# A streaming encoder step on one core: the pair that is finished last stays on chip, three pairs are stored twice, and their splits move two products back

## The chip, the cores and the metric

The kernel runs on one core of one Trainium2 chip. The metric is the device time of one execution in microseconds (us). Five engines work side by side, each through its own queue in order: TensorE (PE) multiplies, VectorE (DVE) and ScalarE (ACT) do elementwise work, GpSimd (POOL) does elementwise work and issues transfers of its own, SyncE (SP) only issues transfers. An instruction that waits holds up everything behind it in its queue.

## The reference, cut to what matters

One layer over 640 tokens (512 of the prompt, 128 of the samples), model width 2048, all in float32. The change lies in the feed-forward part:

```
D_FF = -(-8 * D_MODEL // (3 * 256)) * 256        # 5632
h = rmsnorm(x, norm_ffn)
return x + (jax.nn.silu(h @ w_gate) * (h @ w_up)) @ w_down
```

The projection, the two kinds of attention and the output projection ahead of it are not touched.

## The kernel before

**Arithmetic.** Float32 values are multiplied as two rounded parts, hi and lo: ACT writes hi (a copy that rounds), DVE or POOL writes lo = value - hi (a *split*), and PE adds the three products hi·hi, lo·hi and hi·lo (`mm3`, lines 204 to 206). A weight block is split by line 195 (ACT) and 196 (DVE) into one of three pairs of buffers, so the split for a product can be made once PE is through the product three places ahead of it.

**A quartet.** A matrix product of 2 x 2 blocks is done in seven block products instead of eight (Strassen's scheme in Winograd's form). `quartet` loads four weight blocks on SP (line 933), forms their combinations (lines 946 and 948 on DVE, 951 and 960 on POOL) and yields the products in the order p1, p6, p7, p2, p5, p4, p3. They use the left-hand operand numbers ("which") 0, 1, 2, 4, 3, 5, 6. Line 970 adds the results up on DVE.

**FF1.** The 5632 columns are 22 *pairs* of 128-blocks. For each pair one quartet computes the gate and one the up projection. A product has 8 k-tiles, so 24 matmuls. Then lines 1057 to 1059 apply SiLU, 1063 multiplies gate and up, and 1067 to 1070 form the combinations, so that a pair has seven *parts*, one for each product of FF2. `store_part`, called after most products, takes one part: line 1011 writes hi into one of two scratch buffers `half`, 1013 makes lo in place, and 1014 and 1015 store both to `act_d` in DRAM. Pairs 1, 2 and 3 (`raw_pairs`) are not split here: line 1007 stores the part as it is to `first_d`.

**FF2.** There are 32 steps. Step t works on output blocks t % 8 and t % 8 + 8, and on the five or six pairs that are active: pair j is active for 8 steps from START[j] on (modulo 32). With five pairs a product has 15 matmuls and a step 105. The operands of a pair are loaded with line 977 (POOL) as soon as a buffer is free, from `act_d`. In the first eight steps lines 1100 and 1101 load the residual blocks (`x2_d`, shown as `x_d` in the profile). 62 buffers "S" of 640 columns hold all of that; in FF1 56 of them hold the operand h.

**Between FF1 and FF2.** Step 0 uses pairs 0 to 4. After each product of the last up quartet `free` gives back the eight buffers of h that it used, and starts loading that product's operands for step 0: pairs 1 to 3 from `first_d` (line 987, one transfer of 320 KB and one of 160 KB), which it splits at once (992 on ACT, 993 on DVE or POOL), and pairs 0 and 4 with line 977. Pair 21 is finished last and first used in step 23; its parts are split and stored by `store_part` after the products of step 0. Pairs 1 to 3 are needed again in the last steps: line 1093, emitted where they leave (steps 2, 3 and 5) but placed on SP as soon as an operand is split, stores their 21 operands to `act_d`.

**The order.** The program is emitted in this order, and a scheduler then sets the order within each engine. `keep_behind` adds order edges: instructions that were emitted inside a marked stretch (`behind`) stay after the last ACT instruction emitted ahead of it outside of such stretches.

Of the kernel before, what the change touches and what calls it, by code (L numbers as in the profile page):

```python
# [8 lines left out]
ALU = mybir.AluOpType  # L9
# [8 lines left out]
HT = 320  # L18
# [9 lines left out]
REL = 128  # L28
NPAIR = NFF // 2
STEPS = 32  # L30
START = [25, 27, 28, 30, 31, 1, 3, 4, 6, 7, 8, 9, 11, 12, 14, 15, 16, 17, 19, 20, 22, 23]


def active(step):

    return [j for j in range(NPAIR) if (step - START[j]) % STEPS < 8]
# [5 lines left out]
def f(ap):  # L42
    return ap.bitcast(F32)
# [6 lines left out]
class Net:  # L50


    def __init__(self, nc, tc, io, pools):
        self.nc, self.tc, self.io, self.pools = nc, tc, io, pools
        self.uid = 0
        self.lists = {"S": [f"S{i}" for i in range(N_S)], "W": [f"W{i}" for i in range(N_W)]}
        self.owner, self.turns = {}, {}
        self.queues, self.active, self.turn = {}, {}, 0
        self.streams = (("heads 0", "heads"),)
        self.rate, self.due = 1.0, 0.0  # L60
        self.side, self.spread, self.held, self.behind = [], {}, [], []

    def nm(self, s):
        self.uid += 1
# [90 lines left out]
    def keep_behind(self):  # L155

        info = mybir.DependencyInfo(mybir.DependencyClass.NoSync, mybir.DependencyReason.DATA)
        for k, block in enumerate(self.nc.cur_f.blocks):
            inside = [0] * (len(block.instructions) + 1)
            for a, b in self.behind:  # L160
                if k < len(a):
                    inside[a[k]:b[k]] = [1] * (b[k] - a[k])
            last = None
            for i, ins in enumerate(block.instructions):
                if ins.engine == mybir.EngineType.Activation:
                    if not inside[i]:
                        last = ins
                    elif last is not None:
                        self.tc.add_manual_dep(ins, last.name, info, reason="behind")

    def keep_held(self):

# [123 lines left out]
def r(ap):  # L296
    return ap.bitcast(F32R)


def build(nc, tc, io, pools):  # L300
# [673 lines left out]
    def fetch(j, which):  # L974
        t = n.get("S")
        hl = pack(t, HT)
        nc.gpsimd.dma_start(out=r(sh(t, 2, HT)), in_=r(act_d[which, :, j]))  # L977
        lefts[j][which] = t, hl

    raw_pairs = active(0)[1:4]  # L980

    def free(which):
        n.put("S", *(h[which][0] for h in hs))
        for j in raw_pairs[::2]:
            k = min(2, raw_pairs[-1] + 1 - j)
            raw = n.get("S")
            dma(out=sh(raw, k, HT), in_=first_d[which, :, j - raw_pairs[0]:j - raw_pairs[0] + k])
            for a in range(k):
                t = n.get("S")
                hi, lo = hl = pack(t, HT)  # L990
                part = raw[:, a * HT:a * HT + HT]
                nc.scalar.activation(hi, part, AF.Identity)
                (nc.vector, nc.gpsimd)[a].tensor_tensor(lo, part, f(hi), ALU.subtract)
                lefts[j + a][which] = t, hl
            n.put("S", raw)
        for j in active(0):
            if j not in raw_pairs:
                fetch(j, which)

    parts = []  # L1000

    def store_part():

        if parts:
            j, which, src, done = parts.pop(0)
            if j in raw_pairs:
                dma(out=first_d[which, :, j - raw_pairs[0]], in_=src)
            else:
                at = n.emitted()
                hi = n.scratch()  # L1010
                nc.scalar.activation(r(hi), src, AF.Identity)  # L1011
                n.behind.append((at, n.emitted()))
                nc.vector.tensor_tensor(r(src), src, hi, ALU.subtract)  # L1013
                dma(out=act_d[which, :, j, 0], in_=hi)
                dma(out=act_d[which, :, j, 1], in_=src)
            n.put("S", *done)

    gate = None
    for i in range(NPAIR):
        for src in ("w_gate", "w_up"):  # L1020
# [5 lines left out]
            for step, bank in quartet(8, load, hs, (lambda w: next(prep)) if start else None, free if end else None,  # L1026
# [15 lines left out]
                    add(c21, c21, bank)  # L1042
                elif step == "p3":
                    add(c12, c12, bank)
                if step != "p1":
                    store_part()
            if start:
                for _ in prep:
# [12 lines left out]
            else:  # L1061
                for x, g in zip(y, gate):
# [7 lines left out]
                tt(s4, c12, s2, ALU.subtract)  # L1070
                parts = [(i, 0, c11, [y[0]]), (i, 1, s2, []), (i, 6, s4, [w]), (i, 2, s3, []),
                         (i, 3, s1, [u]), (i, 4, c12, []), (i, 5, c22, [y[1]])]
                store_part()
    n.put("S", r_f)


# [7 lines left out]
    def step(t, part="all"):  # L1084
# [23 lines left out]
        for name, bank in quartet(cnt, load, [lefts[j] for j in now], None, after, part):  # L1108
# [178 lines left out]
```

## Time and profile before

| | us |
|---|---|
| median of 3 runs (lowest, highest) | 2642.64 (2640.0, 2644.74) |
| the profiled execution's own time | 2642.07 |
| its span, first to last instruction | 2640.3 |
| PE busy | 2573.0 (97%) |
| DVE, ACT, POOL busy | 2009.7, 1094.8, 665.9 |
| mean granted TensorE clock | 0.993 |
| transferred | 388.46 MB, 147 GB/s over the span |

FF1 takes the span from about 937 to 2047 us and FF2 the rest. Times below count from the start of the span. In rows of the timeline, the bracket at the end says how long the engine had been idle before the instruction and what ended that. Short instructions on PE overlap: a matmul lasts 0.31 us from its start to its end, and one starts every 0.146 us at the full clock.

### The profile page before, as it was taken

The page shows a single profiled execution, that of the slowest core. Times are in us where ns is not written, and L with a number is a line of the kernel's source. Part 1 is how long each engine was busy: PE and PEld are TensorE (multiplying, and loading weights), DVE is VectorE, ACT ScalarE, POOL GpSimd, SP SyncE. Part 2 cuts the span into 40 slices and gives each one's busy share as a digit, 9 for nine tenths or more (in the row PEclk, how much of TensorE's full clock was granted, in tenths as well). Part 3 has the DMA queues.
Part 4 walks back from the last instruction along what each step waited for, and adds up shares of the span by engine and source line. Part 5 has one row for each costly group of instructions (what it writes and reads, how often), then busy time and mean ns, then how long its engine had stood idle before and what let it go on. Part 6 is the DMA issues. An engine that isn't in the chain of part 4 may idle for free.

```text
span 2640.3 us, 45009 instructions
## 1 busy us (share of the span) xinstructions
PE 2573.0 (97%) x17437; PEld 2533.6 (96%) x17437; DVE 2009.7 (76%) x3115; ACT 1094.8 (41%) x1776; POOL 665.9 (25%) x577
## 2 busy tenths in 40 slices
PE   8999999999999999999999999999999799999997
PEld 8999998999899999999999999999999799999996
DVE  5775677767866788668888888888887677777797
ACT  5554444445634553333443433333344333333343
POOL 0000000000211213233233233333334433333353
PEclk9999999999999999999999999999999999999998
DMA  5322232434655433333433433433437965666655
GB/s 170 102 72 91 89 103 90 131 117 148 205 188 182 156 122 125 119 100 119 153 125 123 150 123 126 153 117 131 150 115 229 365 197 155 169 184 169 186 156 177
DMA packets 178678, 388.46 MB, mean 147 GB/s; under 512 B 21856, under 2 KB 70496, under 8 KB 178464
## 3 DMA queue, kind: packets, MB, share of 16 engines
q1 hardware_dynamic: 153120, 329.21, 38.6%
q0 software_dynamic: 24192, 55.06, 7.4%
q8 instruction: 137, 2.24, 0.4%
q10 hardware_dynamic: 1152, 1.31, 0.1%
q14 instruction: 77, 0.63, 0.1%
HBM read 301.90 MB, written 82.87 MB: 146 GB/s over the span
## 4 chain that ended last, share of the span: by engine, by line
PE 83%; DVE 7%; DMA 5%; ACT 2%; issue 2%; POOL 0%; SPq 0%; DVEq 0%; ACTq 0%; POOLq 0%
PE dn L206 18%; PE dn L204 18%; PE dn L205 17%; PE at L204 9%; PE at L205 9%; PE at L206 9%; DVE W L196 2%; PE at L321 2%; DMA W<-w_down 2%; PE at L416 1%; DVE S L970 1%; ACT W L195 1%; DMA act_d<-half 1%; PE at L212 1%; PE at L211 1%
## 5 line engine op out<-in xcount | busy, mean ns | idle before, releaser
L206 PE MATMUL dn<-S,W 128*128 128x320 f32 x3694 | 1146.1, 310 | 14.4 <-DVE W L196 14.1
L204 PE MATMUL dn<-S,W 128*128 128x320 f32 x3694 | 1153.6, 312 | 4.5 <-ACT W L195 3.5
L205 PE MATMUL dn<-S,W 128*128 128x320 f32 x3694 | 1144.2, 310 | 1.7 <-DVE S L200 1.3
L195 ACT ACTIVATE W<-W 128x1024 fp32r<-128x1024 f32 (+2 forms) x632 | 608.0, 963 | 978.9 <-PE dn L205 541.3
L196 DVE TENSOR_TENSOR W<-W,W 128x1024 fp32r<-128x1024 f32 (+2 forms) x632 | 737.6, 1167 | 82.9 <-ACT W L195 79.2
L206 PEld LDWEIGHTS dn<-S,W 128*128 128x128 f32 x3694 | 694.6, 188 | 19.4 <-DVE W L196 19.1
L204 PEld LDWEIGHTS dn<-S,W 128*128 128x128 f32 x3694 | 695.3, 188 | 9.3 <-ACT W L195 4.6
L205 PEld LDWEIGHTS dn<-S,W 128*128 128x128 f32 x3694 | 694.9, 188 | 3.7 <-DVE S L200 1.5
L204 PE MATMUL at<-S,W 128*128 128x320 f32 x1594 | 495.2, 311 | 7.0 <-ACT W L195 7.0
L206 PE MATMUL at<-S,W 128*128 128x320 f32 x1594 | 495.7, 311 | 4.0 <-DVE W L196 4.0
L205 PE MATMUL at<-S,W 128*128 128x320 f32 x1594 | 494.5, 310 | 0.0
L951 POOL TENSOR_TENSOR W<-W,W 128x1024 f32<-128x1024 f32 (+2 forms) x75 | 159.2, 2122 | 643.8 <-DVE W L196 482.9
L204 PEld LDWEIGHTS at<-S,W 128*128 128x128 f32 x1594 | 301.0, 189 | 7.8 <-ACT W L195 7.8
L206 PEld LDWEIGHTS at<-S,W 128*128 128x128 f32 x1594 | 300.9, 189 | 6.3 <-DVE W L196 6.3
L205 PEld LDWEIGHTS at<-S,W 128*128 128x128 f32 x1594 | 301.0, 189 | 0.0
L970 DVE TENSOR_TENSOR S<-S,dn 128x320 f32<-128x320 f32 x358 | 163.7, 480 | 69.1 <-PE dn L206 69.0
L960 POOL TENSOR_TENSOR W<-W,W 128x1024 f32<-128x1024 f32 (+2 forms) x75 | 163.9, 2185 | 115.9 <-DVE W L196 110.2
L946 DVE TENSOR_TENSOR W<-W,W 128x1024 f32<-128x1024 f32 (+2 forms) x76 | 122.5, 1612 | 69.4 <-DMA W<-w_down 35.5
L970 DVE TENSOR_TENSOR S<-S,at 128x320 f32<-128x320 f32 x262 | 123.1, 479 | 51.1 <-PE at L206 50.3
L977 POOL DMA_DIRECT2D S<-act_d x168 | 91.7, 547 | 184.3 <-PE dn L206 88.9
L948 DVE TENSOR_TENSOR W<-W,W 128x1024 f32<-128x1024 f32 (+2 forms) x76 | 83.4, 1097 | 67.0 <-DMA W<-w_up 34.7
L1013 DVE TENSOR_TENSOR S<-S,half 128x320 fp32r<-128x320 f32 x133 | 115.1, 886 | 13.0 <-ACT half L1011 11.2
(159 smaller groups left out, 2200.1 us busy)
## 6 DMA issues: line engine op xcount, KB each, us to landing
S<-act_d POOLq DMA_DIRECT2D x168, 320.0 KB, 3.9
W<-w_gate SPq DMA_DIRECT2D x88, 512.0 KB
W<-w_up SPq DMA_DIRECT2D x88, 512.0 KB
W<-w_in SPq DMA_DIRECT2D x66, 512.0 KB
W<-w_down SPq DMA_DIRECT2D x64, 384.0 KB
W<-w_down SPq DMA_DIRECT2D x68, 320.0 KB
act_d<-half SPq DMA_DIRECT2D x133, 160.0 KB
act_d<-S SPq DMA_DIRECT2D x133, 160.0 KB
```

What stands on the lines that cost most here:

```text
L195: self.nc.scalar.activation(hi, src, AF.Identity)
L196: self.nc.vector.tensor_tensor(lo, src, f(hi), ALU.subtract)
L204: mm(out, a[0], b[0], start=first, stop=False)
L205: mm(out, a[0], b[1], start=False, stop=False)
L206: mm(out, a[1], b[0], start=False, stop=last)
L946: nc.vector.tensor_tensor(b12[:, w], b12[:, w], b22[:, w], sub)
L948: nc.vector.tensor_tensor(s6[:, w], b11[:, w], b12[:, w], sub)
L951: eng.tensor_tensor(b11[:, w], b22[:, w], s6[:, w], sub)
L960: eng.tensor_tensor(b21[:, w], b21[:, w], s6[:, w], sub)
L970: add = lambda o, a, b: nc.vector.tensor_tensor(o, a, b, ALU.add)
L977: nc.gpsimd.dma_start(out=r(sh(t, 2, HT)), in_=r(act_d[which, :, j]))
L1013: nc.vector.tensor_tensor(r(src), src, hi, ALU.subtract)
```

## The change

START is rotated so that pair 21, not pair 5, begins in step 1; pair 5 begins in step 3, where pair 6 did, and so on. The parts of pair 21 are not stored: `keep_last` splits them between the products of step 0 straight into operand buffers. Parts of pairs 1 to 3 are stored whole as FF1 forms them, and then also go through `store_part` like those of other pairs; so line 1093 falls away. `free` starts the raw transfers of a product, and the splits of that product are emitted two products later (`split_raws`; those of the last two in step 0). The marked stretches `later` keep them behind on ACT, DVE and POOL.

```diff
-START = [25, 27, 28, 30, 31, 1, 3, 4, 6, 7, 8, 9, 11, 12, 14, 15, 16, 17, 19, 20, 22, 23]
+START = [25, 27, 28, 30, 31, 3, 4, 6, 7, 8, 9, 11, 12, 14, 15, 16, 17, 19, 20, 22, 23, 1]
...
     def free(which):
         n.put("S", *(h[which][0] for h in hs))
+        own = []
         for j in raw_pairs[::2]:
             k = min(2, raw_pairs[-1] + 1 - j)
             raw = n.get("S")
             dma(out=sh(raw, k, HT), in_=first_d[which, :, j - raw_pairs[0]:j - raw_pairs[0] + k])
+            own.append((j, k, raw))
+        fetch_late()
+        raws.append((which, own))
+        late.append(which)
+        if len(raws) > 2:
+            split_raws()
+
+    def fetch_late():
+        for which in late:
+            for j in active(0):
+                if j not in raw_pairs:
+                    fetch(j, which)
+        late.clear()
+
+    def split_raws():
+        at = n.emitted()
+        which, own = raws.pop(0)
+        for j, k, raw in own:
             for a in range(k):
                 t = n.get("S")
                 hi, lo = hl = pack(t, HT)
...
                 (nc.vector, nc.gpsimd)[a].tensor_tensor(lo, part, f(hi), ALU.subtract)
                 lefts[j + a][which] = t, hl
             n.put("S", raw)
-        for j in active(0):
-            if j not in raw_pairs:
-                fetch(j, which)
+        n.later.append((at, n.emitted()))
+
+    def keep_last(which):
+        at = n.emitted()
+        t = n.get("S")
+        hi, lo = hl = pack(t, HT)
+        nc.scalar.activation(hi, kept[which], AF.Identity)
+        (nc.vector, nc.gpsimd)[which % 2].tensor_tensor(lo, kept.pop(which), f(hi), ALU.subtract)
+        lefts[NPAIR - 1][which] = t, hl
+        if not kept:
+            n.put("S", *kept_own)
+        n.later.append((at, n.emitted()))
...
             j, which, src, done = parts.pop(0)
-            if j in raw_pairs:
-                dma(out=first_d[which, :, j - raw_pairs[0]], in_=src)
-            else:
...
-                if step != "p1":
+                if step != "p1" or i - 1 in raw_pairs:
                     store_part()
...
-                store_part()
+                if i == NPAIR - 1:
+                    kept, kept_own, parts = {x[1]: x[2] for x in parts}, y + gate, []
+                elif i in raw_pairs:
+                    for _, which, src, _ in parts:
+                        dma(out=first_d[which, :, i - raw_pairs[0]], in_=src)
+                else:
+                    store_part()
...
         def after(which):
             gone = [j for j in now if j not in nxt]
-            for j in gone:
-                if j in raw_pairs and t < 8:
-                    dma(out=act_d[which, :, j], in_=sh(lefts[j][which][0], 2, HT))
             n.put("S", *(lefts[j][which][0] for j in gone))
-            waiting.append([(j, which) for j in nxt if j not in now])
+            if t == 0:
+                fetch_late()
+                if which in (1, 2):
+                    split_raws()
+                for x in {0: (0,), 2: (1,), 4: (2,), 3: (4,), 5: (3,), 6: (5, 6)}.get(which, ()):
+                    keep_last(x)
+            waiting.append([(j, which) for j in nxt if j not in now and j != NPAIR - 1])
             fetch_waiting(2)
...
             elif name == "p3":
                 add(c12, c12, bank)
-            store_part()
             yield name
```

In `keep_behind`, the loop that knew ACT and `behind` now runs over ACT (with `behind` and `later`), DVE and POOL (with `later`). After the change, lines 195, 196, 946, 951, 960, 970 and 977 are lines 198, 199, 949, 954, 963, 973 and 980; the raw splits are 1016 and 1017, those of pair 21 1027 and 1028.

The first place is ACT in the last up quartet. Before, this is what stands between the weight split for p5 (first row) and that for p4 (last row): the raw splits of which 2 (three rows) and the first two of which 4. W are weight buffers, S activations.

```order
L195 ACTIVATE W2_3230_21659<-W0_3188_21463 128x1024
L992 ACTIVATE S12_3213_21593<-S44_3212_21591 128x320
L992 ACTIVATE S39_3214_21596<-S44_3212_21591 128x320
L992 ACTIVATE S43_3216_21601<-S45_3215_21599 128x320
L992 ACTIVATE S26_3224_21642<-S34_3223_21640 128x320
L992 ACTIVATE S5_3225_21645<-S34_3223_21640 128x320
L195 ACTIVATE W10_3240_21707<-W7_3219_21609 128x1024
```

Now, from the weight split for p5 to that for p4:

```order
L198 ACTIVATE W2_3243_21742<-W0_3209_21568 128x1024
L1016 ACTIVATE S34_3240_21731<-S27_3217_21635 128x320
L1016 ACTIVATE S26_3241_21734<-S27_3217_21635 128x320
L1016 ACTIVATE S5_3242_21737<-S35_3218_21637 128x320
L1016 ACTIVATE S20_3250_21781<-S28_3225_21674 128x320
L1016 ACTIVATE S51_3251_21784<-S41_3226_21676 128x320
L198 ACTIVATE W10_3253_21790<-W7_3232_21692 128x1024
```

Five splits stand there as before, but they are those of which 1 (three rows) and the first of which 2, whose transfers start one product earlier than those of which 2 and 4.

The second place is POOL in the same quartet, up to the combination that the product p4 takes (the last row): W7 is the weight block, and once it is done W1's buffer is free, which is where SP loads the first w_down block that step 0 uses. Before:

```order
L1059 TENSOR_TENSOR S8_3162_21266<-S8_3162_21266,S36_1958_11112 128x640
L977 DMA S2_3198_21511<-act_d_7811 128x640
L977 DMA S57_3206_21556<-act_d_7811 128x640
L977 DMA S10_3207_21558<-act_d_7811 128x640
L977 DMA S20_3218_21606<-act_d_7811 128x640
L993 TENSOR_TENSOR S48_3203_21548<-S28_3201_21543,S48_3203_21548 128x320
L960 TENSOR_TENSOR W7_3219_21609<-W7_3219_21609,W1_3189_21466 128x1024
```

Now:

```order
L1090 TENSOR_TENSOR S8_3183_21371<-S8_3183_21371,S36_1958_11112 128x640
L980 DMA S40_3220_21641<-act_d_7811 128x640
L980 DMA S48_3227_21678<-act_d_7811 128x640
L980 DMA S57_3228_21680<-act_d_7811 128x640
L1017 TENSOR_TENSOR S4_3230_21685<-S20_3213_21601,S4_3230_21685 128x320
L963 TENSOR_TENSOR W7_3232_21692<-W7_3232_21692,W1_3210_21571 128x1024
```

The raw split ahead of the combination was one of which 1; now it is one of which 0.

The third place is ACT in step 0. Before, splits of pair 21 into the scratch buffers stand between the weight splits, from that for p5 (first row) on to those of step 1:

```order
L195 ACTIVATE W10_3285_21938<-W1_3266_21821 128x640
L1011 ACTIVATE half_3273_21873<-S8_3162_21266 128x320
L1011 ACTIVATE half_3278_21902<-S17_3151_21196 128x320
L195 ACTIVATE W4_3290_21967<-W7_3279_21907 128x640
L1011 ACTIVATE half_3284_21932<-S17_3151_21196 128x320
L195 ACTIVATE W2_3294_21994<-W6_3265_21819 128x640
L1011 ACTIVATE half_3288_21961<-S4_3208_21560 128x320
L195 ACTIVATE W10_3305_22031<-W0_3303_22026 128x640
```

Now, from the split for p5 to the first of step 1:

```order
L198 ACTIVATE W10_3302_22023<-W1_3278_21899 128x640
L1027 ACTIVATE S12_3304_22042<-S2_3221_21643 128x320
L198 ACTIVATE W4_3306_22048<-W7_3297_21996 128x640
L1027 ACTIVATE S39_3308_22067<-S17_3172_21301 128x320
L198 ACTIVATE W2_3309_22071<-W6_3277_21897 128x640
L1027 ACTIVATE S58_3311_22090<-S2_3221_21643 128x320
L1027 ACTIVATE S22_3312_22093<-S8_3183_21371 128x320
L198 ACTIVATE W10_3321_22112<-W0_3319_22107 128x640
```

The splits of pair 21 stand at like places, but write into buffers "S" of which each is used once, where the two scratch buffers went round.

More of the change, by code (lines that the diff above doesn't have):

```diff
@@ L60, in __init__ @@
         self.rate, self.due = 1.0, 0.0
-        self.side, self.spread, self.held, self.behind = [], {}, [], []
+        self.side, self.spread, self.held, self.behind, self.later = [], {}, [], [], []
     def nm(self, s):
@@ L980, in build @@
     raw_pairs = active(0)[1:4]
+    raws, late, kept, kept_own = [], [], {}, []
     def free(which):
         n.put("S", *(h[which][0] for h in hs))
+        own = []
         for j in raw_pairs[::2]:
@@ L1005, in store_part @@
             j, which, src, done = parts.pop(0)
-            if j in raw_pairs:
-                dma(out=first_d[which, :, j - raw_pairs[0]], in_=src)
-            else:
[L1009 to L1015, printed above, removed]
+            at = n.emitted()
+            hi = n.scratch()
+            nc.scalar.activation(r(hi), src, AF.Identity)
+            n.behind.append((at, n.emitted()))
+            nc.vector.tensor_tensor(r(src), src, hi, ALU.subtract)
+            dma(out=act_d[which, :, j, 0], in_=hi)
+            dma(out=act_d[which, :, j, 1], in_=src)
             n.put("S", *done)
```

25 lines of the change are left out of this document (14 added, 11 removed).

## The prediction

> **What bounds the kernel now.** The page's first part comes first.
>
> ```profile
> PE 2573.0 (97%) x17437; PEld 2533.6 (96%) x17437; DVE 2009.7 (76%) x3115; ACT 1094.8 (41%) x1776; POOL 665.9 (25%) x577
> ```
>
> PE is the bound; only time in which it stands or runs slowly can be won. The busy table by stretches shows where that is around the place of the change. Behind the stretch and its length come PE, PEld, DVE, ACT and POOL (the number behind x counts PE's matmuls), then the granted clock, the DMA share and GB/s.
>
> ```profile
> 2000.00:2020.00 20.00, 19.84 (x136) 19.61 (x135) 14.44 (x20) 7.97 (x12) 5.59 (x4) 1.00 0.56 173
> 2020.00:2040.00 20.00, 15.89 (x96) 15.10 (x94) 13.48 (x17) 8.09 (x16) 14.59 (x16) 0.89 1.00 329
> 2040.00:2060.00 20.00, 16.05 (x97) 15.06 (x97) 16.97 (x24) 8.95 (x18) 15.76 (x21) 0.94 1.12 392
> 2060.00:2080.00 20.00, 10.33 (x48) 8.47 (x46) 8.85 (x17) 4.74 (x9) 4.40 (x9) 0.83 1.14 389
> 2080.00:2100.00 20.00, 19.77 (x125) 19.77 (x126) 14.96 (x23) 6.93 (x11) 6.12 (x5) 0.92 0.99 332
> 2100.00:2120.00 20.00, 18.24 (x123) 17.75 (x122) 12.88 (x20) 6.39 (x10) 7.33 (x8) 1.00 0.93 307
> 2120.00:2140.00 20.00, 20.00 (x138) 20.00 (x137) 16.56 (x27) 6.99 (x10) 5.28 (x6) 1.00 0.57 159
> ```
>
> The last stretch is undisturbed and has 138 matmuls. The six before it have 625 of 828: 203 are missing, at 0.146 us (343 matmuls in 50 us, quoted in part 5) each **29.7 us**. That is all that can be won here. PE's timeline names what it stood for:
>
> ```profile
> 2034.54 0.41 PE L204 MATMUL at<-S,W 128*128 128x320 f32 x1 [2.08 <-ACT W L195]
> 2036.90 0.64 PE L206 MATMUL at<-S,W 128*128 128x320 f32 x1 [1.80 <-DVE W L196]
> 2048.76 0.41 PE L206 MATMUL dn<-S,W 128*128 128x320 f32 x1 [1.34 <-DVE W L196]
> 2053.27 0.39 PE L204 MATMUL dn<-S,W 128*128 128x320 f32 x1 [2.34 <-ACT W L195]
> 2067.68 0.63 PE L204 MATMUL at<-S,W 128*128 128x320 f32 x1 [4.46 <-ACT W L195]
> 2074.98 0.41 PE L206 MATMUL dn<-S,W 128*128 128x320 f32 x1 [1.26 <-DVE W L196]
> 2080.23 0.64 PE L206 MATMUL dn<-S,W 128*128 128x320 f32 x1 [2.79 <-DVE W L196]
> 2107.84 0.41 PE L206 MATMUL dn<-S,W 128*128 128x320 f32 x1 [1.75 <-DVE W L196]
> ```
>
> It is always a weight split. These gaps sum to 17.8 us; the slow clock (0.11+0.06+0.17+0.08 of 20 us) makes 8.4 more, smaller gaps the rest. Matmuls at 0.64 instead of about 0.40 us show where the clock had fallen: after 4.46, after 2.79, after 2.08 and 1.80 together, but not after 2.34 alone.
>
> What held the splits, on ACT:
>
> ```profile
> 2013.71 0.47 ACT L992 ACTIVATE S<-S 128x320 fp32r<-128x320 f32 x1 [5.83 <-DMA act_d<-S]
> ...
> 2029.76 0.83 ACT L992 ACTIVATE S<-S 128x320 fp32r<-128x320 f32 x2 [2.61 <-DMA S<-first_d]
> ...
> 2066.53 0.47 ACT L1011 ACTIVATE half<-S 128x320 fp32r<-128x320 f32 x1 [7.65 <-DMA act_d<-half]
> ...
> 2072.00 0.47 ACT L1011 ACTIVATE half<-S 128x320 fp32r<-128x320 f32 x1 [4.37 <-DMA act_d<-half]
> ```
>
> In FF1 ACT stands for the buffer of a raw split or for raw parts that have not landed, in step 0 for a scratch buffer whose store is under way; the weight split queues behind. All of these are waits for transfers, and the table shows transfers at 392 and 389 GB/s from 2040 to 2080.
>
> **Part 1: transfers that go.** The issues between 2020 and 2110, and, as the last row, between 2200 and 2400; the number at the end is the median time to landing:
>
> ```profile
> S<-act_d POOLq DMA_DIRECT2D x38, 320.0 KB, 7.2
> act_d<-S SPq DMA_DIRECT2D x20, 320.0 KB
> ...
> act_d<-half SPq DMA_DIRECT2D x7, 160.0 KB
> ...
> S<-act_d POOLq DMA_DIRECT2D x54, 320.0 KB, 3.5
> ```
>
> The 21 stores of line 1093 (20 of them here) go, the 14 half-size stores of pair 21 (7 of hi, 7 of lo) go, and so do 7 loads of pair 5 for step 1, as pair 21 needs none: 21+7+7 = 35 times 320 KB, 11.5 MB, 29 us at 392 GB/s. Loads of operands and of w_down remain.
>
> **Part 2: splits two products behind (the last up quartet).** Ahead of p4's weight split ACT now waits at most for which 1 and the first of which 2, whose transfers start one product (24 x 0.146 = 3.5 us) earlier. That exceeds the 2.61 us it stood, so this gap goes. Next late is the DVE half of the same split:
>
> ```profile
> 2026.28 1.55 POOL L993 TENSOR_TENSOR S<-S,S 128x320 fp32r<-128x320 f32 x1 [0.88 <-ACT S L992]
> 2027.80 3.38 POOL L960 TENSOR_TENSOR W<-W,W 128x1024 f32<-128x1024 f32 x1
> 2031.20 0.33 SPq L933 DMA_DIRECT2D W<-w_down  x1
> 2034.89 0.83 DVE L948 TENSOR_TENSOR W<-W,W 128x640 f32<-128x640 f32 x1 [1.18 <-DMA W<-w_down]
> 2035.63 1.22 DVE L196 TENSOR_TENSOR W<-W,W 128x1024 fp32r<-128x1024 f32 x1
> ```
>
> POOL's combination frees a weight buffer, SP loads w_down into it at once, step 0's combination that needs this block stands on DVE ahead of p4's split, and PE goes on at 2036.90. The quartet begins at 2013.8, so p4, its sixth product, is due 5 x 3.5 us later, at 2031.4. POOL no longer waits for which 1 but for which 0, one product earlier: 2036.9 - 3.5 = 2033.4, 2.0 us late. ACT's wait of 5.83 us at the quartet's beginning goes too, as its raw split has moved; if 2 us of it reach this chain, p4 is in time. I take **0.5 us**, nearer to that, with bounds 0 and 3.3 (of the 5.5 us that p4 is late now, only the ACT gap of 2.08 goes).
>
> **Part 3: step 0.** The ACT waits of 7.65 and 4.37 us go, as the scratch buffers aren't used. Splits of pair 21 stay, 7 on ACT, 4 on DVE and 3 on POOL; the 21 raw ones are as many as before. DVE gets tight next. From the landing of that w_down block on it does, in order, up to the split for p7 of step 0: a combination and two multiplications (0.83), two weight splits of FF1 (1.22) and three of FF2 (0.82), 8 activation splits (0.49) and 6 additions (0.48).
>
> ```profile
> 2047.89 0.81 DVE L196 TENSOR_TENSOR W<-W,W 128x640 fp32r<-128x640 f32 x1
> ...
> 2052.69 0.48 DVE L970 TENSOR_TENSOR S<-S,dn 128x320 f32<-128x320 f32 x1
> ...
> L993 DVE TENSOR_TENSOR S<-S,S x14: 479/493/1864, 2014.2 to 2048.9; 128x320 fp32r<-128x320 f32 x14
> ...
> L993 POOL TENSOR_TENSOR S<-S,S x7: 860/898/1549, 2018.5 to 2046.7; 128x320 fp32r<-128x320 f32 x7
> ```
>
> That is 14.2 us, near 13 as neighbours overlap by 0.08 (L948 above ends after L196 begins). Begun at 2029 (2034.9 less 3.5 and some of the 5.83) it ends at 2042; the quartet ends at 2013.8 + 24.6 = 2038.4, and p7 is due two products of 2.2 us later, at 2042.8. With so little slack POOL counts: the same DVE split takes 0.49 us at the median and up to 1.86 (min/median/max in ns above). POOL has a combination, a split and a subtraction of pair 21 in this stretch, some 4 us by the rows here and in part 4, of which DVE may lose none or all. I take **2.5 us**, bounds 0 and 5.
>
> **Part 4: steps 1 and 2.** Step 1's first weight block is loaded when POOL's second combination of step 0 is done.
>
> ```profile
> L977 POOL DMA_DIRECT2D S<-act_d x168 | 91.7, 547 | 184.3 <-PE dn L206 88.9 <-PE at L206 73.3 <-DVE W L946 8.0
> ...
> L1068 POOL TENSOR_TENSOR S<-S 128x320 f32<-128x320 f32 x22 | 39.1, 1776 | 16.6 <-DVE S L1063 16.6
> L960 POOL TENSOR_TENSOR W<-W,W 128x640 f32<-128x640 f32 x16 | 26.2, 1639 | 27.1 <-DVE W L196 21.4 <-DMA W<-w_down 5.7
> ```
>
> Ahead of it now stand two subtractions of pair 21 (1.8 and 0.9), a raw split and one of pair 21 (0.9 each) and five load issues (0.55): 7.3 us, with its own 1.6 8.9. Begun 1.5 us into the step, when DVE has multiplied pair 21, it ends 10.5 us into it. With 4 us to land, a combination, a weight split (0.8 each) and two additions the first product can begin at 17, where a step of 15.4 us that lost some 0.5 ends at 16. I take **1.5 us**, bounds 0 and 3.5 (landing in 7.2 instead of 3.5). For step 2's gap of 1.75 us, also a late w_down, **0.5 us**, bounds 0 and 2.
>
> **Part 5: FF1.** Two stretches, of raw pairs and of others:
>
> ```profile
> 1100.00:1150.00 50.00, 50.00 (x343) 50.00 (x342) 34.69 (x40) 16.98 (x18) 15.78 (x9) 1.00 0.34 108
> 1200.00:1250.00 50.00, 50.00 (x343) 50.00 (x342) 42.17 (x46) 19.50 (x25) 16.70 (x9) 1.00 0.40 131
> ```
>
> Pairs 1 to 3 now do what the second row shows, plus 7 stores of 160 KB in 49 us. PE has its 343 matmuls in both: it hides the splits. New is that line 1044's subtraction in place waits until the raw store has read the part; behind it on DVE stand the weight splits and additions that PE waits for. The store is issued about a product (3.5 us) ahead, and weight splits run two products (7 us, less 1.2 for themselves) ahead, so some 9 us are covered. I take **0**, bounds 0 and 3 (1 us for each of the three pairs).
>
> **Sum.** 29.7 - 0.5 - 2.5 - 1.5 - 0.5 = 24.7. No wait left exceeds 2.5 us, so no slow clock is charged. From the profiled execution's 2642.07 that is 2617.4; it lies 0.57 under the median, so 2618. With all lower bounds 2613; with all upper ones (16.8 us) and one fall of the clock (0.08 x 20 us, as from 2080 on) 2631.
>
> **A rule weighed.** DVE's 1.86 us agrees with the Trainium skill, "SBUF — State Buffer", section "Who interferes with whom": a DVE instruction with two SBUF inputs contends with a GpSimd instruction that reads SBUF, and whichever comes later waits for the whole of the other. It speaks against splits on POOL while DVE is this full. By the rule to the full the time is the second rival's, by the median row alone it is 2615.
>
> **Rivals.**
> - *Transfers stay slow.* Loads of residual blocks and of pairs 5 and 6 start earlier into the freed bandwidth, and landing stays at 7.2 instead of 3.5 us. For: the loads of step 0 alone are 7 x 1.15 MB, 20 us at 392 GB/s within a quartet of 24.6. Against: 11.5 MB go. Four waits (p4, p2 of step 0, first products of steps 1 and 2) each some 3.3 us longer: 2618 + 13 = 2631.
> - *DVE becomes the bound.* From the quartet's end to step 1 POOL has two combinations, five splits and two subtractions, 10.5 us. If DVE loses all of it instead of the 2.5 charged: 2626.
> - *The waits only move.* ACT, DVE and POOL stand for which 5 and 6 ahead of step 0's weight splits, as they stood for scratch buffers: 2643. For: the same queues. Against: these parts are issued some 8 us before their turn.
> - *Slower.* Line 1044 in FF1: 21 waits with weight splits behind them. If a store lands only after the 9 us of cover, each further us costs 21: from 1.2 us beyond the gain is eaten, at 1.6 the time is 2652. For: 7.65 us of waiting for a store were seen. Against: that was at 390 GB/s, here it is 131.
>
> **Chances.** Forecast (2612 to 2623) 0.62, slow transfers 0.18, DVE 0.11, waits moved 0.05, slower 0.04. The range 2612 to 2630 takes in the forecast, DVE and half of the slow transfers, 0.82. A measurement of this kernel tells some 0.2% (5.3 us) from no change: faster 0.91, within 0.05, slower 0.04.
>
> **What would show it.** Right: over 131 matmuls in every stretch of 20 us from 2000 on, no wait for a scratch buffer's store after 2020, landing near 4 us, a clock of 1.00 throughout, FF1 still at 343 per 50 us. Part 2 is wrong if PE stands at p4 for over 3 us; part 3 if DVE has idle time through step 0 while PE waits for line 199; part 5 if FF1 shows fewer than 343. Transfers at 390 GB/s up to 2080 would make the first rival true.

## The result and the profile after

| | before | changed |
|---|---|---|
| median, us (lowest to highest, runs) | 2642.23 (2640.0 to 2644.74, 4) | 2623.27 (2621.49 to 2623.83, 4) |
| span of the profiled execution | 2640.3 | 2619.7 |
| ratio, 95% interval | | 0.993 (0.9918 to 0.9943) |

The change takes 19.0 us off, 0.7%. The forecast was 2618, from 2612 to 2630: the time lies in the range, and the gain was put between 5 and 6 us too high. The busy table of the changed kernel, with the stretches and columns of before:

```profile
2000.00:2020.00 20.00, 20.00 (x139) 20.00 (x138) 17.40 (x21) 8.85 (x14) 7.54 (x6) 1.00 0.68 204
2020.00:2040.00 20.00, 19.05 (x128) 18.52 (x128) 19.97 (x24) 10.25 (x20) 16.50 (x22) 1.00 1.09 370
2040.00:2060.00 20.00, 14.67 (x95) 13.65 (x94) 19.00 (x25) 7.39 (x16) 14.22 (x20) 1.00 1.12 395
2060.00:2080.00 20.00, 18.34 (x122) 17.62 (x121) 16.78 (x26) 7.61 (x11) 5.16 (x4) 1.00 0.50 152
2080.00:2100.00 20.00, 20.00 (x138) 20.00 (x137) 14.05 (x22) 7.31 (x11) 7.34 (x8) 1.00 0.80 230
2100.00:2120.00 20.00, 20.00 (x139) 20.00 (x138) 16.39 (x27) 6.99 (x10) 5.28 (x6) 1.00 0.55 153
```

PE has 761 of 828 matmuls here, where it had 625. At 0.146 us each 9.8 us are still lost of 29.6: 19.9 us are won, and the spans differ by 20.6. So all but 0.7 us of the difference stems from this place. DVE, the third busy time, is now full from 2020 to 2060 (19.97 and 19.00 of 20 us). What PE still stands for, in its timeline:

```profile
2032.28 0.41 PE L209 MATMUL at<-S,W 128*128 128x320 f32 x1 [0.95 <-DVE W L199]
...
2044.30 0.38 PE L207 MATMUL dn<-S,W 128*128 128x320 f32 x1 [2.75 <-ACT S L1027]
...
2051.71 0.42 PE L209 MATMUL at<-S,W 128*128 128x320 f32 x1 [2.17 <-DVE W L199]
...
2061.99 0.38 PE L207 MATMUL dn<-S,W 128*128 128x320 f32 x1 [0.88 <-ACT W L198]
...
2065.47 0.39 PE L207 MATMUL dn<-S,W 128*128 128x320 f32 x1 [0.66 <-ACT W L198]
```

These are p4 of the last quartet, p6 and p2 of step 0, and the first two products of step 1; p5 of step 0 has 0.37 us more. (Each gap costs some 0.16 us beyond its bracket, which counts from the end of a matmul.) The transfers from 2020 to 2110, in 40 slices of 2.25 us, and the loads of operands (count, size, median to landing):

```profile
GB/s 304 323 365 387 397 389 387 385 391 385 391 395 404 393 394 396 396 398 389 265 39 138 140 0 164 127 39 239 165 277 225 306 213 178 289 140 150 239 296 186
...
S<-act_d POOLq DMA_DIRECT2D x35, 320.0 KB, 6.7
```

Up to 2063 (19 slices) they run at 304 to 404 GB/s, then fall off; before, every stretch of 20 us up to 2120 had over 300 GB/s. FF1 is as it was, with 343 matmuls from 1100 to 1150 and from 1200 to 1250.

### The profile page after: what moved, and what is told of

Its sections match the earlier page's. It is cut to its first block, busy times and chain, and to the rows that moved or that the text cites. A ratio compares the mean times of both kernels' runs of the same rounds, so it can differ in the third digit from the quotient of the medians.

```text
span 2619.7 us, 45100 instructions
## 1 busy us (share of the span) xinstructions
PE 2565.2 (98%) x17437; PEld 2527.9 (96%) x17437; DVE 2027.7 (77%) x3133; ACT 1101.9 (42%) x1797; POOL 663.8 (25%) x573
## 4 chain that ended last, share of the span: by engine, by line
PE 85%; DVE 8%; DMA 3%; ACT 2%; issue 2%; POOL 0%; SPq 0%; DVEq 0%; ACTq 0%; POOLq 0%
PE dn L209 18%; PE dn L207 18%; PE dn L208 18%; PE at L207 9%; PE at L208 9%; PE at L209 9%; DVE W L199 2%; PE at L324 2%; DMA W<-w_down 1%; PE at L419 1%; DVE S L973 1%; ACT W L198 1%; PE at L215 1%; PE at L214 1%; ACT S L440 0%
## 5 line engine op out<-in xcount | busy, mean ns | idle before, releaser
L209 PEld LDWEIGHTS dn<-S,W 128*128 128x128 f32 x3694 | 694.1, 188 | 10.5 <-DVE W L199 10.1
```

What stands on the lines that cost most here:

```text
L209: mm(out, a[1], b[0], start=False, stop=last)
```

## The experiments

Each ran beside the kernel before, on the same chip as it; differences are between medians. "Lost" is 828 less the matmuls from 2000 to 2120, times 0.146 us; what it falls by agrees with the measured difference within 2.3 us for every kernel, so that little goes elsewhere. It is taken from the one execution that was profiled, which for `x_dve` was its fastest and for `x_dve_evac` its slowest.

| kernel | median, us (range, runs) | against before | ratio, 95% interval | matmuls | lost, us |
|---|---|---|---|---|---|
| stores_back | 2631.60 (2629.51 to 2637.02, 5) | -9.9 | 0.9952 to 0.9977 | 693 | 19.7 |
| raw_only | 2632.41 (2629.77 to 2635.85, 5) | -9.7 | 0.9948 to 0.9975 | 692 | 19.9 |
| no_lag | 2627.50 (2623.18 to 2628.48, 5) | -14.0 | 0.9931 to 0.9955 | 731 | 14.2 |
| lag_only | 2639.69 (2635.53 to 2644.4, 11) | -2.4 | 0.9981 to 0.9998 | 636 | 28.0 |
| all_dve | 2621.33 (2617.82 to 2622.27, 5) | -19.6 | 0.9914 to 0.9938 | 765 | 9.2 |
| all_pool | 2629.35 (2628.06 to 2629.7, 4) | -11.6 | 0.9942 to 0.9973 | 702 | 18.4 |
| evac_first | 2624.68 (2619.43 to 2625.35, 5) | -16.3 | 0.9922 to 0.9947 | 752 | 11.1 |
| x_late | 2620.31 (2617.67 to 2622.45, 5) | -20.6 | 0.9911 to 0.9936 | 768 | 8.8 |
| x_dve | 2618.61 (2615.27 to 2622.44, 4) | -22.9 | 0.9899 to 0.9926 | 788 | 5.8 |
| x_dve_evac | 2620.63 (2619.18 to 2622.49, 5) | -20.9 | 0.9905 to 0.9932 | 768 | 8.8 |
| x_dve_comb | 2617.60 (2613.37 to 2619.9, 4) | -24.5 | 0.9890 to 0.9917 | 796 | 4.7 |
| after_again | 2622.36 (2622.05 to 2625.64, 5) | -19.7 | 0.9913 to 0.9938 | 756 | 10.5 |

The first four take the change apart; the next four ask what is left; the last four put the answers together. `all_dve`, `all_pool`, `evac_first` and `x_late` were timed together (kernel before: 2640.93), so were `x_dve`, `x_dve_evac`, `stores_back` and `no_lag` (2641.54), and the rest (2642.09). The three groups ran on three chips.

### The stores of the raw pairs, put back

```diff
+            for j in gone:
+                if j in raw_pairs and t < 8:
+                    dma(out=act_d[which, :, j], in_=sh(lefts[j][which][0], 2, HT))
             n.put("S", *(lefts[j][which][0] for j in gone))
```

> The 21 stores of 320 KB of the raw pairs' parts that the change took out are issued again (they write what is there already). 6.9 MB, 17 us of transfers at 390 GB/s. Theory that the gain is the stores': the transfers last to about 2078 instead of 2060, waits return at the starts of steps 1 and 2: 4 to 10 us slower than the changed kernel. Rival, the gain is the lag's or the kept pair's: within 2 us of it.

It costs 9 to 10 us, the upper end. From 2060 to 2080 the transfers run at 361 GB/s, where the changed kernel has 152. In this kernel's timeline DVE waits at step 1's first combination for a w_down block; behind that on DVE stands the weight split for the last product of step 0, and PE waits for it.

```profile
2064.98 0.83 DVE L949 TENSOR_TENSOR W<-W,W 128x640 f32<-128x640 f32 x1 [8.21 <-DMA W<-w_down]
...
2066.99 0.63 PE L209 MATMUL dn<-S,W 128*128 128x320 f32 x1 [7.45 <-DVE W L199]
```

### Pair 21 not kept

```diff
-START = [25, 27, 28, 30, 31, 3, 4, 6, 7, 8, 9, 11, 12, 14, 15, 16, 17, 19, 20, 22, 23, 1]
+START = [25, 27, 28, 30, 31, 1, 3, 4, 6, 7, 8, 9, 11, 12, 14, 15, 16, 17, 19, 20, 22, 23]
...
-                if i == NPAIR - 1:
-                    kept, kept_own, parts = {x[1]: x[2] for x in parts}, y + gate, []
-                elif i in raw_pairs:
+                if i in raw_pairs:
...
-                for x in {0: (0,), 2: (1,), 4: (2,), 3: (4,), 5: (3,), 6: (5, 6)}.get(which, ()):
-                    keep_last(x)
...
+            store_part()
             yield name
```

> The change without the kept pair: pair 21 starts at its old step, its parts go through the scratch buffers and are stored in step 0, and pair 5 is loaded for step 1. Raw pairs and the lag as changed. Theory 'waits for scratch stores and transfers': ACT stands for scratch buffers again in step 0 and 4.5 MB more move (11 us at 390 GB/s): 4 to 8 us slower than the changed kernel, 11 to 15 us under the kernel before. Rival, pair 21's splits only trade places (7 on ACT and 7 on DVE or POOL either way): within 2 us of the changed kernel.

9 to 10 us slower than the changed kernel, a little over what was expected. The trace shows the wait of the kernel before again: a weight split (for p4 of step 0) stands on ACT behind a part that waits for the store of a scratch buffer. That store is late among the other transfers, and this kernel also moves 4.5 MB more; the two were not taken apart.

```profile
2062.39 0.47 ACT L1042 ACTIVATE half<-S 128x320 fp32r<-128x320 f32 x1 [9.96 <-DMA act_d<-half]
...
2063.53 0.63 PE L207 MATMUL at<-S,W 128*128 128x320 f32 x1 [6.05 <-ACT W L198]
```

### Splits right behind their loads

```diff
-        if len(raws) > 2:
-            split_raws()
+        split_raws()
...
-                if which in (1, 2):
-                    split_raws()
```

> Raw splits right behind their load, as before, all else of the change kept. Forecast's part 2: the waits ahead of p4 of the last quartet come back on ACT (2.08 and 1.80 us before), 3 to 5 us slower than the changed kernel. Rival: the freed transfers alone bring the parts in time, or DVE sets the end in both: within 1.5 us.

5 to 6 us slower than the changed kernel: a little over the range named. At p4 PE stands 3.54 us for ACT's weight split (2.08 before), and the clock falls (0.63 us for a matmul):

```profile
2033.27 0.63 PE L207 MATMUL at<-S,W 128*128 128x320 f32 x1 [3.54 <-ACT W L198]
```

### The lag alone, on the kernel before

The change without the kept pair, the whole raw pairs and their second storing; against the kernel before:

```diff
+        fetch_late()
+        raws.append((which, own))
+        late.append(which)
+        if len(raws) > 2:
+            split_raws()
...
+            if t == 0:
+                fetch_late()
+                if which in (1, 2):
+                    split_raws()
```

> The kernel before with nothing but the splits two products behind their loads. Theory 'each part is worth what its own wait was' (forecast's part 2): the gaps of 2.08 and 1.80 us in the last quartet and the slow clock behind them go, 3 to 6 us under the kernel before; the rest stays. Rival 'the transfers after it set the pace': what is won ahead of step 0 is lost again at the waits for stores, 0 to 2 us under.

Nearly the rival: 2.4 us. The interval, from 0.02% to 0.19% (0.5 to 5 us), does not exclude the theory; the trace speaks for the rival. The last quartet is as quick as hoped (132 matmuls from 2020 to 2040, 96 before), and the time is handed over to a store in step 0:

```profile
2060.50 0.47 ACT L1045 ACTIVATE half<-S 128x320 fp32r<-128x320 f32 x1 [10.40 <-DMA act_d<-half]
...
2062.29 0.63 PE L209 MATMUL at<-S,W 128*128 128x320 f32 x1 [11.30 <-DVE W L199]
```

The three parts taken out one at a time cost 9 to 10, 9 to 10 and 5 to 6 us, 23 to 26 together, and the change is worth 19 to 20. An excess of 4 to 6 us is no more than the intervals leave open, but the last trace shows how it comes about: the waits stand one behind another on the same path, and what one part wins, a later wait takes back as long as that wait is there.

### All splits on DVE, or all on POOL

```diff
-                (nc.vector, nc.gpsimd)[a].tensor_tensor(lo, part, f(hi), ALU.subtract)
+                nc.vector.tensor_tensor(lo, part, f(hi), ALU.subtract)
...
-        (nc.vector, nc.gpsimd)[which % 2].tensor_tensor(lo, kept.pop(which), f(hi), ALU.subtract)
+        nc.vector.tensor_tensor(lo, kept.pop(which), f(hi), ALU.subtract)
```

For `all_pool` it is `nc.gpsimd` in both places.

> All splits of raw pairs and of pair 21 on DVE (7 raw and 3 of pair 21 leave POOL). Theory 'DVE is full and POOL holds it': DVE gains 10 x 0.41 = 4 us of work between 2018 and 2060, but the stretched instructions (about 14 us over their undisturbed lengths in that stretch) lose the share that lies beside POOL's splits, some 8 us; the PE gaps there fall by 2 to 4 us, time 2619 to 2621. Rival 'transfers land too late': DVE is only busy because it has slack, time stays within 1.5 us of 2623. Third: DVE's work alone counts, without holding: 2625 to 2628.

> All splits of raw pairs and of pair 21 on POOL (14 raw and 4 of pair 21 leave DVE). If only DVE's own work counts: 18 x 0.41 = 7 us less on DVE, time 2617 to 2620. If POOL holds DVE: POOL gets 18 x 0.9 = 16 us more where it is 16.5 of 20 us busy, its combinations and load issues come later and DVE is held as long: 2628 to 2640. Transfers too late: unchanged, 2623.

All on POOL loses 7 to 8 us against the changed kernel, within what was expected if POOL holds DVE. But most of that loss is not the hold, it is POOL's own queue: POOL is busy for 41.45 of the 42 us from 2018 to 2060, its combination for p4 of step 0 comes only behind the splits, and ACT, PE and DVE (6.08 us) all stand for it.

```profile
2059.19 1.52 POOL L963 TENSOR_TENSOR W<-W,W 128x640 f32<-128x640 f32 x1
...
2060.74 0.74 ACT L198 ACTIVATE W<-W 128x640 fp32r<-128x640 f32 x1 [9.71 <-POOL W L963]
...
2061.53 0.64 PE L207 MATMUL at<-S,W 128*128 128x320 f32 x1 [6.09 <-ACT W L198]
```

All on DVE gave nothing that the time can tell from the changed kernel. The hold itself shows in the lengths of DVE's instructions. DVE's groups from 2018 to 2060 (count, busy time in us and mean in ns), in the changed kernel:

```profile
L1017 DVE TENSOR_TENSOR S<-S,S 128x320 fp32r<-128x320 f32 x14 | 14.8, 1082 | 0.0
L199 DVE TENSOR_TENSOR W<-W,W 128x640 fp32r<-128x640 f32 x7 | 8.0, 1137 | 0.0
L199 DVE TENSOR_TENSOR W<-W,W 128x1024 fp32r<-128x1024 f32 x4 | 6.1, 1530 | 0.6 <-ACT W L198 0.6
...
L973 DVE TENSOR_TENSOR S<-S,dn 128x320 f32<-128x320 f32 x6 | 2.8, 475 | 0.0
```

and with all splits on DVE:

```profile
L1017 DVE TENSOR_TENSOR S<-S,S 128x320 fp32r<-128x320 f32 x21 | 13.5, 675 | 0.0
L199 DVE TENSOR_TENSOR W<-W,W 128x640 fp32r<-128x640 f32 x7 | 7.1, 1011 | 0.0
```

21 operand splits take less of DVE than 14 did. Undisturbed a split takes 0.479 us (the median of line 1017) and a weight split 0.81 or 1.21 (those at 2037.32 and 2034.59, with no elementwise work on POOL beside them); over these, lines 1017 and 199 of the changed kernel are stretched by 14 x 0.603 + 7 x 0.327 + 4 x 0.32 = 12.0 us. Over all lines, the 13 DVE instructions that took at least 0.3 us longer than the shortest of their kind make 14.5 us, and each of the 13 overlaps an elementwise instruction of POOL. With all on POOL, the wide weight split takes twice its time:

```profile
L199 DVE TENSOR_TENSOR W<-W,W 128x1024 fp32r<-128x1024 f32 x4 | 10.1, 2527 | 0.8 <-ACT W L198 0.8
```

Line 973, which adds a PSUM bank to an SBUF buffer, keeps its 0.47 to 0.48 us in all these kernels. The Trainium skill, "SBUF — State Buffer", section "Who interferes with whom", says just that: a DVE instruction with two SBUF inputs contends with a GpSimd instruction that reads SBUF, and one with at most one SBUF input, outside the modes that use both of DVE's ports, does not. The trace agrees on both halves.

With DVE relieved, PE lost nothing up to 2040 (139 matmuls from 2020), and its gaps at p6 and p2 of step 0 are 1.62 and 1.33 us. From 2020 to 2060 that is 18 matmuls (2.6 us) more than in the changed kernel; PE then stood at the start of step 1 instead. SP issued the block of that step's first product at 2051.30 (the first of three issues in this row), ACT had it after 9.9 us, and the clock fell to 0.91 (2060 to 2080):

```profile
2051.30 4.48 SPq L936 DMA_DIRECT2D W<-w_down  x3
...
2061.17 0.74 ACT L198 ACTIVATE W<-W 128x640 fp32r<-128x640 f32 x1 [7.42 <-DMA W<-w_down]
...
2061.96 0.41 PE L207 MATMUL dn<-S,W 128*128 128x320 f32 x1 [3.38 <-ACT W L198]
```

### Additions ahead of splits

```diff
-            split_raws()
+            todo.append(split_raws)
...
                 if step != "p1" or i - 1 in raw_pairs:
                     store_part()
+                while todo:
+                    todo.pop(0)()
```

The same for the splits of step 0.

> Splits are emitted behind the additions of the same product, not ahead of them. Theory: PE stood 2.75 us at 2044.30, when the addition of line 973 for the last product of FF1 ended (2043.72 + 0.47), 4.4 us after that product, behind a multiplication, a weight split and three operand splits; ahead of the splits it ends by 2042.0 and the gap falls under 1 us: 2620 to 2622, if nothing behind the splits gets late by as much. Rival (the row names ACT's line 1027 as what ended the gap): gap and time unchanged, 2623.

A miss. The gap at p6 fell to 1.66 us only (p6 still began 0.1 us after that addition), and gaps of 1.48 and 1.40 us came later in step 0. The median is some 3 us above the changed kernel's, but the intervals overlap, two of the five runs (2619.43, 2620.18) are below all of the changed kernel's, and the profile is of the slowest. So no gain is shown, and no clear loss; in this profile another order on a full DVE only moved the waits.

### Residual loads later

```diff
+            if which == 3 and t < 7:
+                load_x(t + 1)
...
+        dma(out=x, in_=x2_d[q])
+        dma(out=y, in_=x2_d[q + 8])
+        n.slow.append((at, n.emitted()))
```

with order edges that keep these issues on SP behind the w_down loads of the step before.

> The loads of residual blocks for steps 1 to 7 are issued behind the w_down loads of the step before, so that about 12 x 320 KB (10 us at 390 GB/s) leave the crowded stretch from 2033 to 2060. Theory 'transfers land too late': the w_down load of step 1, 6.7 us from issue to landing, lands in about 4, the two gaps of 0.88 and 0.66 us at the start of step 1 go and so does part of the ones before: 2619 to 2621. Theory 'DVE is full': only the 1.5 us at the start of step 1 can go, the gaps of 2.75 and 2.17 stay: 2621.5 to 2623.5.

The time is not to be told from the changed kernel's (their intervals overlap). The gaps fit neither theory in full: 1.75 us at p4 of the last quartet and 2.63 at p6 stay, as the second has it, but the one at p2 is gone, and the clock is at 0.91 from 2040 to 2060. At the start of step 1 the 0.88 us is gone (0.26 us stand at the product before it), and 0.66 is as before.

### Both limits together

`x_dve` has the diffs of `all_dve` and `x_late`, `x_dve_evac` that of `evac_first` too.

> Both edits together: splits on DVE alone, and residual loads of steps 1 to 7 behind the step before. Theory 'two limits in series' (POOL's hold on DVE up to step 1, then the landing of step 1's w_down behind the other transfers): the gaps of 0.95, 2.17 and 0.37 us go as with splits on DVE, the 3.38 us at the start of step 1 that showed there goes as with late loads; some 2 to 4 us stay lost between 2000 and 2100 of about 10: 23 to 26 us under the kernel before of the same call. Rival 'each edit saves the same time': as with late loads alone, 20 to 21 us under it.

> The two edits, and splits emitted behind the additions of their product. If the gap of 1.6 to 2.7 us at the second product of step 0 is the wait for the addition of line 973 behind the splits, it goes under 1 us: 1 to 2 us faster than the two edits without it. If later splits make later products wait, as they did alone, no gain or 1 to 2 us slower.

Together the two edits are 22.9 us under the kernel before, just short of the 23 to 26 hoped for, and the interval overlaps those of each edit alone. In the profiled run, 3.3 us below the median, 5.8 us are lost, where each alone left some 9: gaps of 2.21 us at p6 and 0.95 at p2 of step 0 stay, and the 3.38 us at the start of step 1 have become 0.81 and 0.72. With the order of additions changed too there is no gain: 2 us slower, within the intervals.

```diff
-                                      eng=nc.vector if start else nc.gpsimd):
+                                      eng=nc.vector if start or end else nc.gpsimd):
...
-        for name, bank in quartet(cnt, load, [lefts[j] for j in now], None, after, part):
+        for name, bank in quartet(cnt, load, [lefts[j] for j in now], None, after, part,
+                                  nc.vector if t == 0 else nc.gpsimd):
```

> Splits on DVE, residual loads late, and the combinations of the last quartet of FF1 and of step 0 on DVE instead of POOL (0.8 to 1.2 us each on DVE, 1.6 to 2.4 on POOL, which holds DVE as long). Theory of the hold: DVE is free sooner, 0.5 to 2 us faster than with the first two edits alone, 23 to 25 us under the kernel before. Rival, DVE's own work counts: 1 to 3 us slower than the two edits, 20 to 22 under.

> The changed kernel as it is, beside the others: 18 to 20 us under the kernel before, gaps of 0.95, 2.75, 2.17, 0.37, 0.88 and 0.66 us again at the same places within 0.3 us each. If they differ by more, single gaps of a run are chance and only sums by stretch can be compared.

`x_dve_comb` (these lines and `x_dve`) is the fastest: 2617.60, 4.8 us under the changed kernel timed beside it, with all four runs below all five of that. It lies in the range of its theory (23 to 25 us under the kernel before), though its interval overlaps that of `x_dve`. Its DVE is all but undisturbed, as line 1017 shows (0.540 us in the mean):

```profile
L1017 DVE TENSOR_TENSOR S<-S,S 128x320 fp32r<-128x320 f32 x21 | 10.6, 540 | 1.8 <-ACT S L1016 1.8
```

The second profile of the changed kernel has the same sum (10.5 and 9.8 us lost) but other gaps: 1.96, 1.14, 2.19 and 0.64 us for 0.95, 2.75, 2.17 and 0.66, none of 0.25 us or more for the 0.37 and 0.88, and 3.6 us of slow clock. So the hope of the same gaps within 0.3 us failed. A single gap of one profile is good to a microsecond or so, no more.

## Why the forecast held, and where it was 5 us off

- **29.7 us at stake:** right (203 x 0.146 is 29.6). All but 0.7 us of what was won was won there, and 9.8 us are left instead of 5.0.
- **Part 1, transfers that go:** right. Put back, the 21 stores alone cost 9 to 10 us, and pair 21's stores and loads with their scratch buffers as much. But landing was assumed at 4 us in part 4, and the loads of operands took 6.7 in the median from 2020 to 2110, little less than the 7.2 before.
- **Part 2, p4:** 0.95 us for 0.5, 2.0 in the second profile; within its bounds. The reason given, a late w_down block, was the smaller part: in the first profile the block is in time, since DVE does line 951 at 2029.59 without idling, and in the second DVE idles 0.75 us for it; DVE itself is full.
- **Part 3, step 0:** this step failed. It charged 2.5 us (0 to 5); PE stands 2.75 + 2.17 + 0.37 = 5.3 (in the second profile 1.14 + 2.19, and 1.8 of slow clock). It let DVE begin its 14.2 us of work at 2029 with slack behind it, and put POOL's part at 4 us at most. But with ACT's waits gone DVE is busy from 2018 on (40.81 of 42 us up to 2060), and its instructions are stretched by 14.5 us beside POOL's, 12 of them in the two lines above. How a gap arises is seen in the changed kernel's DVE and POOL rows ahead of p6 and of p2:

```profile
2038.57 1.91 DVE L1094 TENSOR_TENSOR S<-S,S 128x640 f32<-128x640 f32 x1
2040.40 1.52 DVE L199 TENSOR_TENSOR W<-W,W 128x640 fp32r<-128x640 f32 x1
2041.85 1.15 DVE L1017 TENSOR_TENSOR S<-S,S 128x320 fp32r<-128x320 f32 x1
2042.91 0.48 DVE L1028 TENSOR_TENSOR S<-S,S 128x320 fp32r<-128x320 f32 x1
2043.32 0.48 DVE L1017 TENSOR_TENSOR S<-S,S 128x320 fp32r<-128x320 f32 x1
2043.72 0.47 DVE L973 TENSOR_TENSOR S<-S,dn 128x320 f32<-128x320 f32 x1
...
2048.53 2.39 DVE L1017 TENSOR_TENSOR S<-S,S 128x320 fp32r<-128x320 f32 x1
2050.85 0.81 DVE L199 TENSOR_TENSOR W<-W,W 128x640 fp32r<-128x640 f32 x1
...
2038.22 1.57 POOL L954 TENSOR_TENSOR W<-W,W 128x640 f32<-128x640 f32 x1 [0.98 <-DVE W L199]
...
2040.34 0.89 POOL L1017 TENSOR_TENSOR S<-S,S 128x320 fp32r<-128x320 f32 x1
2041.18 1.47 POOL L1099 TENSOR_TENSOR S<-S 128x320 f32<-128x320 f32 x1
...
2048.87 0.89 POOL L1101 TENSOR_TENSOR S<-S,S 128x320 f32<-128x320 f32 x1
2049.71 0.86 POOL L1028 TENSOR_TENSOR S<-S,S 128x320 fp32r<-128x320 f32 x1
```

  The first three would take 0.82, 0.81 and 0.48 us; beside POOL's three they take 2.5 us more, nearly the whole gap of 2.75. PE goes on 0.10 us after the addition of line 973, which reads a bank `dn`, as p6 writes one. The gap of 2.17 us at p2 ends with the weight split at 2050.85; the operand split ahead of it took 1.9 us more than its 0.48, beside POOL's two at 2048.87 and 2049.71.

  The forecast also misread the wait at p6. It took every gap before for a weight split, and so counted this one among the time that goes with ACT's waits. But in the kernel before p6 (2053.27, 2.34 us) began 0.10 us after line 970's addition too (2052.69 + 0.48, a row of the forecast), where PE began 0.05 us after ACT's split at 2034.54 and 2067.68. ACT's split had ended at the same moment as the addition, so that trace alone does not decide; the 0.10 us came back in all 13 other traces.
- **Part 4:** 0.88 + 0.66 us at step 1 for 1.5, none at step 2 for 0.5; right in sum, and in part by luck: the load took 6.7 us from its issue at 2053.42, not 4, and was covered because step 0 had itself become 5 us longer. Once step 0 was quicker (`all_dve`) the gap of 3.38 us appeared.
- **Part 5, FF1:** right, 343 matmuls per 50 us.
- **No slow clock:** right in one profile; the second shows 0.91 in two stretches of 20 us.
- **Its own signs:** FF1 and the scratch stores came out as said. But 131 matmuls were missed in three of six stretches (128, 95, 122), landing was 6.7 us, not 4, and transfers ran near 390 GB/s up to 2063.
- **The rivals:** DVE as the bound (2626) was the mechanism, but it adds 3 us at step 0 (5.3 for 2.5), not 8. The time, 2623.27, is nearer to it than to 2618, and just outside the forecast's own 2612 to 2623; the stated range held because it took in this rival. Slow transfers (2631) were true of the landing, but cost one short wait instead of four. The waits that only move are what the lag alone does. Line 1044 cost nothing.

What is shown: POOL's elementwise work stretches DVE's, and the kernel that takes nearly all of that away (line 1017: 0.540 us for 1.082) and loads the residuals later is 4.8 us faster. That kernel holds three edits, and no smaller set is told from the changed kernel with certainty, so what POOL's hold and the landing of step 1's block each cost is argued from the gaps, not measured. In the best kernel p6 still begins 0.10 us after line 973's addition (1.55 us of idling), on a DVE that is busy 38.72 of 42 us: DVE's own work is left there. The rest of its 4.7 us was not followed up.

## What to carry to other kernels

When several waits stand one behind another on one path, no part of a change has a price of its own: count what the last of them leaves. A part put in alone can then be worth less than its own wait, and the parts taken out one by one can cost more than the whole. When a wait goes, add up the work of the engine that waited beside it over the whole stretch, with its durations as they are beside its neighbours, not at their median. Work put on GpSimd to spare VectorE can cost VectorE more than doing it there: with ten splits taken off GpSimd, VectorE did 14 more instructions from 2018 to 2060 in less busy time (39.22 us for 40.81). And it lengthens GpSimd's own queue, where the combinations for later products stand.

## What was not expected of the hardware

- The profile's name for what ended a gap can mislead. In the changed kernel and all twelve experiments p6 of step 0 began 0.10 us after the end of line 973's addition on DVE, while the rows name a line of ACT (198, 1016, 1027, 1147, 1148, 1151 or 1160) or "issue"; ACT's last end lay anywhere from 0.01 to 0.58 us back.
- A DVE split of 0.48 us took 4.55 us, while POOL did a split and a combination that began after it had (2019.99 by the trace):

```profile
L1017 DVE TENSOR_TENSOR S<-S,S x14: 477/479/4547, 2020.0 to 2048.5; 128x320 fp32r<-128x320 f32 x14
...
2020.58 0.91 POOL L1017 TENSOR_TENSOR S<-S,S 128x320 fp32r<-128x320 f32 x1
2021.43 2.43 POOL L963 TENSOR_TENSOR W<-W,W 128x1024 f32<-128x1024 f32 x1
```

  So the starts in a trace do not tell who waits for whom: by "whichever comes later waits", the rule weighed in the forecast, the split would have gone first. Whether its start as shown is the moment at which it got its operands is not shown.
- The clock doesn't follow the longest gap: in the second profile it fell after 1.96 us (a matmul of 0.51 us), in the first it did not after 2.75 (0.38 us). Cut more finely, the second profile has the clock at a half for 3.41 us from 2034.61 and again from 2055.09, which is six times 3.41 later; in the 3.41 us ahead of each fall PE stood for 1.96 and 2.07 us. On a grid of the same period, laid from such a fall at 688.20 in the first profile, the gap of 2.75 us is cut into 1.74 and 1.01. PE's busy time and the clock (second column behind the stretch, third last) in two cells of the second profile and one of the first:

```profile
2031.20:2034.61 3.41, 1.45 (x10) 1.18 (x9) 2.96 (x4) 1.12 (x3) 2.37 (x5) 1.00 1.17 392
2034.61:2038.02 3.41, 3.41 (x14) 3.41 (x15) 3.41 (x6) 1.10 (x2) 1.59 (x3) 0.50 1.16 390
...
2039.88:2043.29 3.41, 1.67 (x12) 1.41 (x10) 3.41 (x4) 2.78 (x7) 2.74 (x3) 1.00 1.12 387
```

  From 1900 to 2139, 13 of the 14 traces fit a simple rule: a cell with 1.96 us of idling or more was followed by a fall from the full clock, one with 1.81 or less was not. In `x_dve_evac` the clock fell after 1.45.
- With the stores put back, SP's issues waited for SP's own earlier transfers, 1.65 us apart (2043.96, 2045.61, 2047.31), so w_down loads were issued late as well as landing late (2052.29, 2058.45 and 2061.80, for 2047.04, 2053.42 and 2056.45 in the changed kernel). The waits on SP in that kernel from 2040 to 2070 (total, times, longest):

```profile
SPq L1130 <- DMA act_d<-S: 3.8, 3, 1.3
SPq L1130 <- DMA W<-w_down: 2.7, 2, 1.4
```

  Whether that is a limit on transfers under way was not tried.
